# Operands at multiples of 512 bytes, value blocks of 512 columns, and masks in one run, in a two-layer block kernel

## The chip, the cores and the metric

The kernel runs on one core of one Trainium2 chip. The time is the device time of that core in microseconds (us). TensorE (PE in the profile) multiplies, VectorE (DVE) and ScalarE (ACT) do the elementwise work, GpSimd (POOL) a few small operations, and SyncE (SP) issues the transfers. SBUF is the working memory, PSUM the memory that TensorE accumulates in.

## The reference

Two transformer layers over 256 tokens of 1024 features in float32, batch 1. In the first, neighbourhood attention and three-group dilated attention are merged by sigmoid gates, a layer of 16384 experts follows, and a gated embedding. In the second, a multi-scale pooling stands beside differential attention, and a gated convolutional layer ends it.

```python
# first layer
h = rms_norm(x, norm_mix)
qa, ka, va, qd, kd, vd, gate_na, gate_dil = split(h @ w_in)       # va 512 columns, vd 768
out_na = neighbourhood_attention(norm(qa), norm(ka), va, bias)    # 8 heads of 64
out_dil = dilated groups (128,1), (512,4), (2048,16), 4 heads of 64 each, joined by their softmax sums
x = x + (sigmoid(gate_na) * (out_na @ w_na) + sigmoid(gate_dil) * (out_dil @ w_dil)) @ w_out
x = x + peer_ffn(rms_norm(x, norm_ffn))                           # top 16 of 128 x 128 keys, 8 heads; experts u and v
x = x + sigmoid(rms_norm(x, norm_ple) @ w_ple_gate) * (p @ w_ple)
# second layer
p, q, k, v = split(rmsnorm(x) @ w_in_2)
attn = softmax(q1 k1) - lam * softmax(q2 k2)                      # 4 heads of 2 x 64, mask by chunks of 64 tokens
x = x + concat(pool(p), norm(attn @ v)) @ w_o
u = causal_conv(rmsnorm(x) @ w_up); x = x + (silu(u_gate) * u_val) @ w_down
return rmsnorm(x)
```

## The kernel before

All features stand on the 128 partitions, all 256 tokens in one tile. Every weight matrix is cut into units of 128 x 1024 (512 KB), which `Stream` loads in the order of the list `units`. ScalarE copies each to `wh` (rounded to fp32r, `wh<-wr`, L126), and VectorE writes the rest to `wl` (L127). `h_hi`, `h_lo` and their likes are the same two parts of an activation. A product is then three fp32r matmuls: high by high, low by high, high by low (`mm3`, L295 to L297). Where features come out, the activation (256 tokens) is the moving operand and 128 columns of the weights are the stationary one, 24 matmuls of 256 columns for a unit (`feature_unit`). Where tokens come out, the weights move, 512 columns at a time, and the activation is stationary, 12 matmuls for a unit (`token_unit`).

The stages follow each other: value blocks, q and k with the heads behind them, gates, branches and `w_out`, query with the top-16 lists, 128 units of `u` (of which the first 8 take the normalized copy `hP`), 128 units of `v` (stationary operand `av`), the embedding, and the second layer. Work that belongs beside a stage (softmax, transposes, routing) is written as generators, which `Background` steps between units. A scheduler then orders each engine's instructions; `Order` adds edges where the author fixes an order.

**Positions.** A tile takes a multiple of 32 bytes of each partition, and the tiles of a pool stand one behind the other. Worked out from the sizes of the tiles: `x`, `wh`, `wl`, `h_hi`, `h_lo`, `qkd`, `qka`, `vv` and the merged projection's `hp_h` start 352 bytes past a multiple of 512 bytes; `av` and the expert stage's `hp_h`, which stand behind the 32-byte tile `sm` (L704), at 384; `mx_h` at 416; `f_h` at 32. Slices of them begin at multiples of 512 bytes within the tile, so all slices of a tile share its position.

**Value blocks** (L571 to L590). Five blocks of 256 columns, two weight units each, accumulate in a tile of `pmm`; ScalarE writes each to `vv`.

**Scores.** `dilated(j)` is one of four heads: a mask of 512 columns is put into PSUM by a bf16 matmul with the identity (L497), and products over 64 rows are added to it (L498 for the first group, 256 keys; L500 for the second and third, 128 keys). Heads 2c and 2c+1 use rows 0 to 63 and 64 to 127. An f32 matmul is two passes in the profile. `neighbourhood(hp)` makes two heads' scores (L540) without a mask matmul, `differential(h)` those of two softmaxes (L1010), each followed by the chunk mask (L1011).

Of the kernel before, what the change touches and what calls it, by code (L numbers as in the profile page):

```python
# [9 lines left out]
F32 = mybir.dt.float32  # L10
# [10 lines left out]
P = 128  # L21
S = 256
# [151 lines left out]
class Order:  # L174
# [11 lines left out]

    def begin(self):
        self.close()
        self.start, self.last = len(self.nc.cur_bb.bb.instructions), {}
# [32 lines left out]
def block_kernel(ctx, tc, nc, a, out, dbg=None):  # L222
# [12 lines left out]

    x = keep.tile([P, 2, D], F32, name="x")
# [23 lines left out]
    nc.vector.tensor_copy(identb, ident)  # L260

# [49 lines left out]
    def rms_rstd(pool):  # L311

        ss = pool.tile([P, 2, 2], F32, name="ss")
        rstd = pool.tile([P, 2], F32, name="rstd")
# [121 lines left out]
    with ExitStack() as ph:  # L436
# [52 lines left out]
        def dilated(j):  # L489
            po, cj = 64 * (j % 2), j // 2  # L490
            yield from pause(PA)
            row = slice(po, po + 64)
            sc = scores()
            for qt in range(2):
                q = slice(qt * P, (qt + 1) * P)
                o = sc[:, qt * 512:(qt + 1) * 512]
                MM(o, lhsT=identb, rhs=mask[:, qt, :], start=True, stop=False)  # L497
                MM(o[:, :S], lhsT=qkd[row, 0, cj, q], rhs=qkd[row, 1, cj, :], start=False, stop=False)  # L498
                for g in (1, 2):
                    MM(o[:, (g + 1) * P:(g + 2) * P], lhsT=qkd[row, 0, 2 * g + cj, q], rhs=qkd[row, 1, 2 * g + cj, q], start=False, stop=g == 2)  # L500
            yield
            mx = wk.tile([P, 8], F32, name="mx")
# [28 lines left out]
        def neighbourhood(hp):  # L531
# [5 lines left out]
            for i in range(4):  # L537
                hh, qt = divmod(i, 2)
                po = 64 * hh
                MM(sc[:, i * S:(i + 1) * S], lhsT=qka[po:po + 64, 0, hp, qt * P:(qt + 1) * P],  # L540
                   rhs=qka[po:po + 64, 1, hp, :], start=True, stop=True)
# [3 lines left out]
            mx = wk.tile([P, 12], F32, name="mxn")  # L545
# [26 lines left out]
        for i in range(5):  # L572
            ps = pmm.tile([P, 2, S], F32, name="mm", tag="mm")
            for kk in range(2):
                w = st.get(None if i or kk else 0)
                for k4 in range(4):
                    k = 4 * kk + k4
                    for t in range(2):
                        MM(ps[:, t, :], lhsT=hT.hi[:, k, t * P:(t + 1) * P], rhs=w.hi[:, k4 * S:(k4 + 1) * S], start=(k == 0 and t == 0), stop=False)
                        MM(ps[:, t, :], lhsT=hT.hi[:, k, t * P:(t + 1) * P], rhs=w.lo[:, k4 * S:(k4 + 1) * S], start=False, stop=False)  # L580
                        MM(ps[:, t, :], lhsT=hT.lo[:, k, t * P:(t + 1) * P], rhs=w.hi[:, k4 * S:(k4 + 1) * S], start=False, stop=k == 7 and t == 1)
                if i == 0 and kk == 0:
                    norm.rest()
            if i == 0:
                rstd = rms_rstd(wk)
            c = (512 + i * S) if i < 3 else (i - 3) * S
            for t in range(2):
                ACT(vv[:, t, c:c + S], ps[:, t, :], AF.Identity, scale=rstd[:, t:t + 1])
            if i == ROWAT:
                run(rescale(wk, token_row(wk, rstd), hP))  # L590
# [7 lines left out]
        for i in range(10):  # L598
            ps = pmm.tile([P, 2, S], F32, name="mm", tag="mm")
            for j in range(2):  # L600
                feature_unit(ps[:, j, :], st.get(), hP)
                if j == LJ:
                    run(late)
                bg.step(STEPS[0])
            raw = wk.tile([P, 2, S], F32, name="raw", bufs=3)
            ACT(raw, ps, AF.Copy)
            sf = wk.tile([P, 2, S], F32, name="sf")
            ACT(sf, ps, AF.Square)
            sq = HL(wk.tile([P, 2, S], F32R, name="sq_h"), wk.tile([P, 2, S], F32R, name="sq_l"))
            split(sq, sf)  # L610
            if i < 6:
                cj, g = divmod(i, 3)
                jobs = [dilated(2 * cj), dilated(2 * cj + 1)] if g == 2 else []
# [44 lines left out]
    with ExitStack() as ph:  # L658
# [45 lines left out]
        sm = big.tile([P, 8], F32, name="sm")  # L704
# [190 lines left out]
    lam = tab.tile([P, 4], F32, name="lam")  # L895
    lamc = lam[:, 3:4]
    lam_init = 0.8 - 0.6 * float(np.exp(-0.0))
    cmb = tab.tile([P, P], BF, name="cmb")
# [3 lines left out]
    def make_tables():  # L902

        invf = tab.tile([P, 1], F32, name="invf")
# [26 lines left out]
        lj = tab.tile([P, 64], F32, name="lj")  # L931
# [55 lines left out]
    with ExitStack() as ph:  # L987
# [14 lines left out]
        def differential(h):  # L1002
            yield from pause(D0)
            base = psc.tile([P, 2, 512], F32, name="sc")
            for qt in range(2):
                e = P * (qt + 1)
                sc = base[:, :, qt * P:qt * P + e]
                for n in range(2):
                    po = 64 * n
                    MM(sc[:, n, :], lhsT=qk[po:po + 64, 0, h, qt * P:(qt + 1) * P], rhs=qk[po:po + 64, 1, h, :e], start=True, stop=False)  # L1010
                    MM(sc[:, n, e - P:], lhsT=identb, rhs=cmb, start=False, stop=True)  # L1011
            yield
            attn = []
            for qt in range(2):
                e = P * (qt + 1)
                sc = base[:, :, qt * P:qt * P + e]
                mx = wk.tile([P, 8], F32, name="mxd")
# [25 lines left out]
            s2 = wk.tile([P, 4], F32, name="s2")  # L1043
# [57 lines left out]
        def rows2():  # L1101
# [6 lines left out]
            rstd = wk.tile([P, 2], F32, name="rstdn")  # L1108
# [38 lines left out]
    with ExitStack() as ph:  # L1147
# [50 lines left out]
        ss = big.tile([P, 2, 2], F32, name="ss_out")  # L1198
        rstd = big.tile([P, 2], F32, name="rstd_out")
# [37 lines left out]
def _blocks(w):  # L1237

    n = w.shape[1]
    return w.reshape(2, 4, P, n // S, S).transpose(3, 0, 2, 1, 4).reshape(n // S * 2, P, 4 * S)  # L1240
# [6 lines left out]
def _arrays(i):  # L1247
# [8 lines left out]
    d["w_v"] = np.concatenate([_blocks(sp[5]), _blocks(sp[2])])  # L1256
# [81 lines left out]
```

## Time and profile before

| | us |
|---|---|
| three runs | 1369.22, 1370.15, 1371.18; median 1370.15 |
| profiled execution, its own time | 1369.19 |
| its span, first to last instruction | 1367.4 |
| TensorE busy | 1352.7 |
| VectorE busy | 1011.0 |
| ScalarE busy | 744.7 |

Busy time counts overlapping instructions once. Matmuls overlap, so the listed length of one is longer than its distance to the next; the distance is read from two starts in the timeline. `PEld` is the loading of stationary operands.

### The profile page before, as it was taken

To read this page: it belongs to the slowest core of one execution; us is meant where nothing else is said; L and a number is where in the kernel's file an instruction comes from. 1 tells how busy PE (TensorE), PEld (TensorE's weight loads), DVE (VectorE), ACT (ScalarE), POOL (GpSimd) and SP (SyncE) were. 2 spreads that over 40 slices of the span, in tenths; PEclk is the share of its full clock that TensorE was granted. 3 is DMA by queue.
4 is the path that set the end of the run, shared out by engine and by line. 5 is a ranking of instruction groups with operands and counts; after the bars stand their busy time and mean duration, and the time that the engine had idled before them with its cause. 6 is when DMAs were issued, how large, how long until landed. Compare 5 with 4: busy or idle time off the path is not lost.

```text
span 1367.4 us, 23920 instructions
## 1 busy us (share of the span) xinstructions
PE 1352.7 (99%) x9312; PEld 1229.9 (90%) x9312; DVE 1011.0 (74%) x1850; ACT 744.7 (54%) x1293; POOL 10.4 (1%) x16
## 2 busy tenths in 40 slices
PE   9999999999999999999999999999999999999997
PEld 8988998999999999999988888888888788999997
DVE  7687557987889988889855555555557686798886
ACT  6657565564545555544544444444446764665554
POOL 0000000000000000000000000000000000000000
PEclk9999999999999999999999999999999999999999
DMA  6534455455555444454555555555575544455551
GB/s 248 186 120 141 151 163 186 147 184 185 184 185 164 157 159 155 157 168 154 166 188 185 185 187 189 192 186 186 188 248 176 173 148 139 165 190 186 187 185 60
DMA packets 66642, 236.03 MB, mean 173 GB/s; under 512 B 7521, under 2 KB 8545, under 8 KB 66401
## 3 DMA queue, kind: packets, MB, share of 16 engines
q1 hardware_dynamic: 66240, 234.32, 52.5%
q8 instruction: 73, 1.20, 0.3%
q14 instruction: 41, 0.33, 0.1%
q10 hardware_dynamic: 288, 0.18, 0.0%
HBM read 233.43 MB, written 1.05 MB: 171 GB/s over the span
## 4 chain that ended last, share of the span: by engine, by line
PE 78%; DVE 2%; ACT 1%; issue 1%; DMA 0%; POOL 0%; POOLq 0%; DVEq 0%; ACTq 0%
PE acc L295 17%; PE acc L297 17%; PE acc L296 17%; PE mm L295 5%; PE mm L297 5%; PE mm L296 5%; PE up L295 3%; PE up L296 3%; PE up L297 3%; PE trg L831 2%; DVE wl L127 1%; PE sc L1010 1%; PE trs L723 1%; ACT wh L126 0%; DMA wr<-in_w_qk_dram 0%
## 5 line engine op out<-in xcount | busy, mean ns | idle before, releaser
L127 DVE TENSOR_TENSOR wl<-wr,wh 128x1024 fp32r<-128x1024 f32 (+2 forms) x435 | 527.3, 1215 | 263.7 <-ACT wh L126 263.4
L126 ACT ACTIVATE wh<-wr 128x1024 fp32r<-128x1024 f32 (+2 forms) x435 | 457.0, 1053 | 460.8 <-PE acc L297 214.7
L295 PE MATMUL acc<-wh,av 128*128 128x512 f32 x512 | 202.7, 396 | 0.0
L296 PE MATMUL acc<-wl,av 128*128 128x512 f32 x512 | 202.5, 396 | 0.0
L297 PE MATMUL acc<-wh,av 128*128 128x512 f32 x512 | 202.5, 395 | 0.0
L295 PE MATMUL acc<-h_hi,wh 128*128 128x256 f32 x640 | 184.9, 289 | 0.6 <-ACT wh L126 0.6
L297 PE MATMUL acc<-h_hi,wl 128*128 128x256 f32 x640 | 181.1, 283 | 0.3 <-DVE wl L127 0.3
L296 PE MATMUL acc<-h_lo,wh 128*128 128x256 f32 x640 | 181.0, 283 | 0.0
L295 PE MATMUL mm<-h_hi,wh 128*128 128x256 f32 x512 | 147.1, 287 | 1.5 <-ACT vp L1094 1.5
L296 PE MATMUL mm<-h_lo,wh 128*128 128x256 f32 x512 | 145.4, 284 | 0.2
L297 PE MATMUL mm<-h_hi,wl 128*128 128x256 f32 x512 | 144.9, 283 | 0.4 <-DVE wl L127 0.4
L295 PEld LDWEIGHTS acc<-h_hi,wh 128*128 128x128 f32 x640 | 122.5, 191 | 0.8 <-ACT wh L126 0.8
L297 PEld LDWEIGHTS acc<-h_hi,wl 128*128 128x128 f32 x640 | 122.3, 191 | 0.5 <-DVE wl L127 0.5
L296 PEld LDWEIGHTS acc<-h_lo,wh 128*128 128x128 f32 x640 | 122.5, 191 | 0.0
L295 PEld LDWEIGHTS acc<-wh,av 128*128 128x128 f32 x512 | 96.2, 188 | 23.3
L297 PEld LDWEIGHTS acc<-wh,av 128*128 128x128 f32 x512 | 96.2, 188 | 23.3
L296 PEld LDWEIGHTS acc<-wl,av 128*128 128x128 f32 x512 | 96.2, 188 | 23.0
L295 PE MATMUL up<-h_hi,wh 128*128 128x256 f32 x352 | 99.6, 284 | 0.5 <-ACT row L369 0.5
L295 PEld LDWEIGHTS mm<-h_hi,wh 128*128 128x128 f32 x512 | 98.0, 191 | 1.9 <-ACT vp L1094 1.7
L297 PE MATMUL up<-h_hi,wl 128*128 128x256 f32 x352 | 99.5, 283 | 0.0
L296 PE MATMUL up<-h_lo,wh 128*128 128x256 f32 x352 | 99.4, 283 | 0.0
L296 PEld LDWEIGHTS mm<-h_lo,wh 128*128 128x128 f32 x512 | 98.1, 192 | 0.6 <-DVE h_lo L354 0.6
(334 smaller groups left out, 2577.9 us busy)
## 6 DMA issues: line engine op xcount, KB each, us to landing
wr<-in_u_dram SPq DMA_DIRECT2D x128, 512.0 KB, 3.5
wr<-in_v_dram SPq DMA_DIRECT2D x128, 512.0 KB, 3.4
wr<-in_w_up_dram SPq DMA_DIRECT2D x44, 512.0 KB, 3.5
wr<-in_w_down_dram SPq DMA_DIRECT2D x22, 512.0 KB, 3.5
wr<-in_w_q_dram SPq DMA_DIRECT2D x20, 512.0 KB, 4.0
wr<-in_w_g_dram SPq DMA_DIRECT2D x16, 512.0 KB, 3.5
wr<-in_w_query_dram SPq DMA_DIRECT2D x16, 512.0 KB, 3.5
wr<-in_w_v_dram SPq DMA_DIRECT2D x9, 512.0 KB, 4.9
```

Source lines behind the costliest of these rows:

```text
L126: self.last = [self.nc.scalar.activation(hi[:, c], r[:, c], AF.Copy).ins, self.nc.vector.tensor_tensor(lo[:, c], r[:, c], hi[:, c].bitcast ...
L127: self.nc.vector.tensor_tensor(lo[:, c], r[:, c], hi[:, c].bitcast(F32), op=OP.subtract).ins]
L295: MM(o, lhsT=l.hi, rhs=r.hi, start=start, stop=False)
L296: MM(o, lhsT=l.hi, rhs=r.lo, start=False, stop=False)
L297: st.product = MM(o, lhsT=l.lo, rhs=r.hi, start=False, stop=stop).ins
L723: MM(p[:, t, j, :], lhsT=qT[:, 2 * i + j, t * P:(t + 1) * P], rhs=kT[:, j, :], start=True, stop=True)
L831: MM(p[:, j, :], lhsT=o[:, 0, j // 2, :, j % 2], rhs=o[:, k, j // 2, :, j % 2], start=k == 2, stop=k == 3)
L1010: MM(sc[:, n, :], lhsT=qk[po:po + 64, 0, h, qt * P:(qt + 1) * P], rhs=qk[po:po + 64, 1, h, :e], start=True, stop=False)
```

## The change

- `even` takes a whole 512 bytes for a small tile and hands out its front; a pool `t1` holds the small tiles of the first stage; `sums` replaces `sm`; two unused tiles named `room` fill up `cst` and `t1`. Worked out from the sizes, the matmul operands named above all start at multiples of 512 bytes then. `ident` (128), `ones` (64) and `identb` (96) stay.
- The value columns come in three blocks of 512, 256 and 512 columns, in tiles of the scores' PSUM pool; a unit of a 512-column block holds two k-slices. `w_v` is cut to match.
- `dilated(cj)` makes the scores of two heads: first the four mask matmuls, then the products, alternating between rows 0 to 63 and 64 to 127. `in_turn` fixes that order. The rest of each head becomes a job of its own, and both jobs start at once.
- `neighbourhood` and `differential` alternate in the same way; in `differential` the four chunk masks come behind the products.

```diff
+    def in_turn(self, ins):
+        for i, j in zip(ins, ins[1:]):
+            self.edge(j.ins, i.ins)
...
+    def even(pool, shape, name, dtype=F32, bufs=None):
+        t = pool.tile([P, 512 // (4 if dtype in (F32, U32) else 2)], dtype, name=name, **({} if bufs is None else {"bufs": bufs}))
+        n = int(np.prod(shape))
+        v = t[:, :n]
...
+    sums = cst.tile([P, 8], F32, name="sums")
+    cst.tile([P, 32], F32, name="room")
...
+        tiny = ph.enter_context(tc.tile_pool(name="t1", bufs=2))
+        tiny.tile([P, 24], F32, name="room")
...
-        def dilated(j):
-            po, cj = 64 * (j % 2), j // 2
+        def dilated(cj):
             yield from pause(PA)
-            row = slice(po, po + 64)
-            sc = scores()
+            both = [scores() for _ in range(2)]
+            ins = []
+            for qt in range(2):
+                for sc in both:
+                    ins.append(MM(sc[:, qt * 512:(qt + 1) * 512], lhsT=identb, rhs=mask[:, qt, :], start=True, stop=False))
             for qt in range(2):
                 q = slice(qt * P, (qt + 1) * P)
-                o = sc[:, qt * 512:(qt + 1) * 512]
-                MM(o, lhsT=identb, rhs=mask[:, qt, :], start=True, stop=False)
-                MM(o[:, :S], lhsT=qkd[row, 0, cj, q], rhs=qkd[row, 1, cj, :], start=False, stop=False)
-                for g in (1, 2):
-                    MM(o[:, (g + 1) * P:(g + 2) * P], lhsT=qkd[row, 0, 2 * g + cj, q], rhs=qkd[row, 1, 2 * g + cj, q], start=False, stop=g == 2)
+                for g in range(3):
+                    for h, sc in enumerate(both):
+                        row = slice(64 * h, 64 * h + 64)
+                        o = sc[:, qt * 512:(qt + 1) * 512]
+                        o, keys = (o[:, :S], slice(0, S)) if g == 0 else (o[:, (g + 1) * P:(g + 2) * P], q)
+                        ins.append(MM(o, lhsT=qkd[row, 0, 2 * g + cj, q], rhs=qkd[row, 1, 2 * g + cj, keys], start=False, stop=g == 2))
+            order.in_turn(ins)
             yield
+            rest = [dilated_rest(2 * cj + h, sc) for h, sc in enumerate(both)]
+            for job in rest:
+                bg.add(job)
+                next(job)
...
-        for i in range(5):
-            ps = pmm.tile([P, 2, S], F32, name="mm", tag="mm")
-            for kk in range(2):
+        for i, (c, n) in enumerate(((512, 512), (1024, 256), (0, 512))):
+            ps = scores()
+            per = 1024 // n
+            for kk in range(KD // per):
                 w = st.get(None if i or kk else 0)
...
-        sm = big.tile([P, 8], F32, name="sm")
+        sm = sums
...
-                    MM(sc[:, n, e - P:], lhsT=identb, rhs=cmb, start=False, stop=True)
+                    ins.append(MM(sc[:, n, :], lhsT=qk[po:po + 64, 0, h, qt * P:(qt + 1) * P], rhs=qk[po:po + 64, 1, h, :e], start=qt == 0, stop=False))
+            for qt in range(2):
+                for n in range(2):
+                    ins.append(MM(base[:, n, 2 * qt * P:(2 * qt + 1) * P], lhsT=identb, rhs=cmb, start=False, stop=qt == 1))
+            order.in_turn(ins)
```

Two places show how TensorE's order moves. The first is the dilated scores of heads 0 and 1 in the q and k stage (`mm` is the projection that the scores stand in, `sc` the scores, `identb` the identity that each mask loads). Before, in the second of two stretches, TensorE has:

```order
L295 MATMUL mm<-hp_h,wh 128x256
L500 MATMUL sc<-qkd 128x128
L497 LDWEIGHTS identb
L497 MATMUL sc<-mask,identb 128x512
L498 MATMUL sc<-qkd 128x256
L500 MATMUL sc<-qkd 128x128 x3
L497 LDWEIGHTS identb
L497 MATMUL sc<-mask,identb 128x512
L498 MATMUL sc<-qkd 128x256
L500 MATMUL sc<-qkd 128x128 x2
L296 MATMUL mm<-hp_l,wh 128x256
```

In the changed program the same stretch, on the same engine, reads:

```order
L313 MATMUL mm<-hp_h,wl 128x256
L525 MATMUL sc<-qkd 128x128 x2
L525 MATMUL sc<-qkd 128x256 x2
L525 MATMUL sc<-qkd 128x128 x4
L311 MATMUL mm<-hp_h,wh 128x256
```

Both masks have left this stretch for the first one, where four pairs of `LDWEIGHTS identb` and the mask matmul now stand behind each other, ahead of two products of 256 and two of 128 columns. The first row of scores here is the third group's. Between the two stretches there were 22 matmuls `mm` before and there are 18 now.

The second place is a differential head's scores in the second layer's q and k stage (`cmb` is the chunk mask). Before, TensorE has:

```order
L295 MATMUL mm<-h_hi,wh 128x256
L1010 MATMUL sc<-qk 128x128
L1011 LDWEIGHTS identb
L1011 MATMUL sc<-cmb,identb 128x128
L1010 MATMUL sc<-qk 128x128
L1011 LDWEIGHTS identb
L1011 MATMUL sc<-cmb,identb 128x128
L1010 MATMUL sc<-qk 128x256
L1011 LDWEIGHTS identb
L1011 MATMUL sc<-cmb,identb 128x128
L1010 MATMUL sc<-qk 128x256
```

In the changed program the same head reads:

```order
L311 MATMUL mm<-h_hi,wh 128x256
L1045 MATMUL sc<-qk 128x128 x2
L1045 MATMUL sc<-qk 128x256 x2
L1048 LDWEIGHTS identb
L1048 MATMUL sc<-cmb,identb 128x128
```

The products of the two softmaxes, one on each half of the rows, now follow each other, and the four masks, of which the first is shown, come behind them.

## Rows read from the trace of the kernel before

**Rows 1.** The page, part 1: engine, busy us (share of the span) and instructions.

```profile
...
PE 1352.7 (99%) x9312; PEld 1229.9 (90%) x9312; DVE 1011.0 (74%) x1850; ACT 744.7 (54%) x1293; POOL 10.4 (1%) x16
```

**Rows 2.** Waits of TensorE, longest total first: who waited for whom, us, times, longest.

```profile
...
PE mm L295 <- ACT vp L1094: 1.5, 1, 1.5
```

**Rows 3.** Groups by line and shape on TensorE: count, then busy us, mean ns.

```profile
...
L295 PE MATMUL acc<-wh,av 128*128 128x512 f32 x512 | 202.7, 396 | 0.0
...
L295 PE MATMUL acc<-h_hi,wh 128*128 128x256 f32 x640 | 184.9, 289 | 0.6 <-ACT wh L126 0.6
...
L295 PE MATMUL mm<-h_hi,wh 128*128 128x256 f32 x512 | 147.1, 287 | 1.5 <-ACT vp L1094 1.5
...
L295 PE MATMUL up<-h_hi,wh 128*128 128x256 f32 x352 | 99.6, 284 | 0.5 <-ACT row L369 0.5
...
L295 PE MATMUL mm<-hp_h,wh 128*128 128x256 f32 x320 | 92.2, 288 | 0.0
```

**Rows 4.** Timeline of TensorE, 256 columns: start us, us, then the instruction.

```profile
...
286.65 0.28 PE L295 MATMUL acc<-hp_h,wh 128*128 128x256 f32 x1
...
297.96 0.28 PE L295 MATMUL mm<-hp_h,wh 128*128 128x256 f32 x1
...
320.89 0.28 PE L295 MATMUL acc<-h_hi,wh 128*128 128x256 f32 x1
...
332.41 0.28 PE L295 MATMUL mm<-h_hi,wh 128*128 128x256 f32 x1
```

**Rows 5.** Timeline of TensorE, 512 columns, two places.

```profile
...
202.26 0.39 PE L295 MATMUL acc<-wh,hp_h 128*128 128x512 f32 x1
...
203.62 0.28 PE L295 MATMUL mm<-ona_h,wh 128*128 128x256 f32 x1
203.73 0.28 PE L296 MATMUL mm<-ona_l,wh 128*128 128x256 f32 x1
...
900.07 0.40 PE L297 MATMUL acc<-wh,av 128*128 128x512 f32 x1
...
903.57 0.40 PE L297 MATMUL acc<-wh,av 128*128 128x512 f32 x1
```

**Rows 6.** Timelines of TensorE and VectorE, scores of the dilated and neighbourhood heads.

```profile
...
66.87 0.39 PE L497 MATMUL sc<-mask,identb 128*128 128x512 bf16 x1
67.19 0.70 PE L498 MATMUL sc<-qkd 64*128 64x256 f32 x2
67.72 0.38 PE L500 MATMUL sc<-qkd 64*128 64x128 f32 x2
...
69.20 0.39 PE L295 MATMUL mm<-hp_h,wh 128*128 128x256 f32 x1
...
72.02 0.49 PE L500 MATMUL sc<-qkd 64*128 64x128 f32 x2
...
75.22 0.39 PE L296 MATMUL mm<-hp_l,wh 128*128 128x256 f32 x1
...
126.90 1.14 PE L540 MATMUL sc<-qka 64*128 64x256 f32 x8
...
70.76 0.68 DVE L484 TENSOR_TENSOR qkd<-qn,r 128x512 f32<-128x512 f32 x1
```

**Rows 7.** Timeline of TensorE, scores of one differential head.

```profile
...
1102.34 0.46 PE L1010 MATMUL sc<-qk 64*128 64x128 f32 x2 [0.17 <-issue]
1102.73 0.23 PE L1011 MATMUL sc<-cmb,identb 128*128 128x128 bf16 x1
...
1103.47 0.70 PE L1010 MATMUL sc<-qk 64*128 64x256 f32 x2
1104.10 0.23 PE L1011 MATMUL sc<-cmb,identb 128*128 128x128 bf16 x1
...
1104.92 0.36 PE L296 MATMUL mm<-h_lo,wh 128*128 128x256 f32 x1
```

**Rows 8.** A window of the query stage, columns as in its first line.

```profile
...
core 0: us, PE busy (x) PEld busy (x) DVE busy (x) ACT busy (x) POOL busy (x), PEclk, DMA share, GB/s
228.00:287.00 59.00, 58.61 (x488) 58.15 (x489) 55.35 (x204) 37.42 (x59) 0.74 (x1) 1.00 0.49 161
```

More of the change, by code (lines that the diff above doesn't have):

```diff
@@ L309, in in_order, with rms_rstd @@
         return ap.rearrange("p (n t) -> p n t", t=2)
-    def rms_rstd(pool):
-        ss = pool.tile([P, 2, 2], F32, name="ss")
-        rstd = pool.tile([P, 2], F32, name="rstd")
+    def rms_rstd(pool, small_pool=None):
+        if small_pool is not None or isinstance(pool, type):
+            own = small_pool or pool
+            ss, rstd = own.tile([P, 2, 2], F32, name="ss"), own.tile([P, 2], F32, name="rstd")
+        else:
+            ss, rstd = even(pool, (2, 2), "ss"), even(pool, (2,), "rstd")
         for n in range(2):
@@ L536, in neighbourhood @@
             sc = scores()
[L537 to L541, printed above, removed]
+            ins = []
+            for qt in range(2):
+                for hh in range(2):
+                    i, po = 2 * hh + qt, 64 * hh
+                    ins.append(MM(sc[:, i * S:(i + 1) * S], lhsT=qka[po:po + 64, 0, hp, qt * P:(qt + 1) * P],
+                                  rhs=qka[po:po + 64, 1, hp, :], start=True, stop=True))
+            order.in_turn(ins)
             yield
@@ L571, in block_kernel @@
         hP = mT = HL(big.tile([P, KD, S], F32R, name="hp_h"), big.tile([P, KD, S], F32R, name="hp_l"))
-        for i in range(5):
-            ps = pmm.tile([P, 2, S], F32, name="mm", tag="mm")
-            for kk in range(2):
+        for i, (c, n) in enumerate(((512, 512), (1024, 256), (0, 512))):
+            ps = scores()
+            per = 1024 // n
+            for kk in range(KD // per):
                 w = st.get(None if i or kk else 0)
-                for k4 in range(4):
-                    k = 4 * kk + k4
+                for kw in range(per):
+                    k, cw = per * kk + kw, slice(kw * n, (kw + 1) * n)
                     for t in range(2):
-                        MM(ps[:, t, :], lhsT=hT.hi[:, k, t * P:(t + 1) * P], rhs=w.hi[:, k4 * S:(k4 + 1) * S], start=(k == 0 and t == 0), stop=False)
-                        MM(ps[:, t, :], lhsT=hT.hi[:, k, t * P:(t + 1) * P], rhs=w.lo[:, k4 * S:(k4 + 1) * S], start=False, stop=False)
-                        MM(ps[:, t, :], lhsT=hT.lo[:, k, t * P:(t + 1) * P], rhs=w.hi[:, k4 * S:(k4 + 1) * S], start=False, stop=k == 7 and t == 1)
+                        mm3(ps[:, t * 512:t * 512 + n], hT[:, k, t * P:(t + 1) * P], w[:, cw], k == 0, k == 7)
                 if i == 0 and kk == 0:
                     norm.rest()
+                if i == 0 and kk == 1:
+                    rstd = rms_rstd(wk, tiny)
+            for t in range(2):
+                ACT(vv[:, t, c:c + n], ps[:, t * 512:t * 512 + n], AF.Identity, scale=rstd[:, t:t + 1])
             if i == 0:
[L585 to L589, printed above, removed]
                 run(rescale(wk, token_row(wk, rstd), hP))
@@ L612, in block_kernel @@
                 cj, g = divmod(i, 3)
-                jobs = [dilated(2 * cj), dilated(2 * cj + 1)] if g == 2 else []
+                jobs = [dilated(cj)] if g == 2 else []
                 late = heads(raw, sq, qkd[:, :, 2 * g + cj, :], QK_DIL, True, jobs)
@@ L1004, in differential @@
             base = psc.tile([P, 2, 512], F32, name="sc")
+            ins = []
             for qt in range(2):
@@ L1009, in differential @@
                     po = 64 * n
-                    MM(sc[:, n, :], lhsT=qk[po:po + 64, 0, h, qt * P:(qt + 1) * P], rhs=qk[po:po + 64, 1, h, :e], start=True, stop=False)
-                    MM(sc[:, n, e - P:], lhsT=identb, rhs=cmb, start=False, stop=True)
+                    ins.append(MM(sc[:, n, :], lhsT=qk[po:po + 64, 0, h, qt * P:(qt + 1) * P], rhs=qk[po:po + 64, 1, h, :e], start=qt == 0, stop=False))
+            for qt in range(2):
+                for n in range(2):
+                    ins.append(MM(base[:, n, 2 * qt * P:(2 * qt + 1) * P], lhsT=identb, rhs=cmb, start=False, stop=qt == 1))
+            order.in_turn(ins)
             yield
@@ L1042, in differential @@
             yield
-            s2 = wk.tile([P, 4], F32, name="s2")
+            s2 = even(wk, (4,), "s2")
             on = wk.tile([P, 2, P], F32, name="on")
```

34 lines of the change are left out of this document (20 added, 14 removed).

## The prediction

> **What bounds the kernel now.** I read the page first, for the engine that is never idle. TensorE is busy 1352.7 us of the span, VectorE 1011.0 [rows 1]. The waits of TensorE come next: the largest entry is 1.5 us in all, in one wait [rows 2]. So the time is the number of matmuls multiplied by the distance from one start to the next, plus the places where TensorE changes its tiling. Busy time does not give that distance, since matmuls overlap: a 256-column matmul is listed with some 285 ns. The timeline does. In the expert stage, 96 matmuls (four units of 24) start between 320.89 and 332.41, which is 120.0 ns each [rows 4]. In the second expert stage fifteen 512-column matmuls take 3.50 us, or 233.3 ns [rows 5]. At the granted clock of 1.00 (the 2.4 GHz level, [rows 8]) the columns alone would take 106.7 and 213.3 ns, so 13 to 20 ns of every matmul are something else.
>
> **Part 1, the positions.** The matmuls do not all have that distance, and the groups differ in nothing but where their operands lie:
> - 256 columns, moving and stationary operand both at 352 past a multiple of 512 bytes: 120.0 ns.
> - 256 columns, moving operand (hP of the second stage) at 384, stationary at 352: 96 matmuls from 286.65 to 297.96, or 117.8 ns [rows 4].
> - 512 columns, moving 352, stationary (av) 384: 233.3 ns.
> - 512 columns, both at 352 (merged projection): six from 202.26 to 203.62, or 227 ns [rows 5].
>
> So position counts. The change puts both operands at 0, a pair that the trace does not hold, and the price must be bounded. For 512 columns the nearest row is the pair with equal positions, 227; the ends are 233.3 (no effect) and 220. For 256 columns the nearest is the pair whose moving operand is a multiple of 128, 117.8; the ends are 120.0 and 113, the distance of the first 256-column matmul behind a 512-column run (203.62 to 203.73, [rows 5]). The 220 is an estimate: the same 6.3 ns over the columns that 113 leaves at 256 columns, 213.3 + 6.3. I take the nearest rows.
> - The 512-column matmuls with av are 3 x 512 [rows 3]: 1536 x (233.3 - 227) = 9.7 us; at the ends 0 and 20.4.
> - The 256-column ones with h and hP: 3 x (640 + 512 + 352 + 320) [rows 3] less the 96 at 384 = 5376, x (120.0 - 117.8) = 11.8 us; at the ends 0 and 37.6. Smaller groups are left out.
>
> The Trainium skill speaks against this part. TensorE: Matmul & The Clock Gate, "Step-by-step: what each phase is for", says that the moving operand and the weight load have read ports of their own, so that loading the next weights takes nothing from the running matmul. By that rule both terms are 0, which is rival A. The trace does not agree: 227 against 233.3 at one width and one moving position.
>
> **Part 2, the value blocks.** Five blocks of 256 columns, two units of 24 matmuls each, cost 240 x 120.0 = 28.8 us. After: 96 of 512 columns and 48 of 256, 96 x 227 + 48 x 117.8 = 27.5. That is -1.3 (bounds: -0.6 with 233.3 and 120.0, -2.3 with 220 and 113). The weight units arrive at the same pace, 512 KB per block-half of some 2.8 us, and the h columns are wanted later than before; waits at the start count as 0.
>
> **Part 3, the scores.** Alternating halves buys nothing by itself. In the neighbourhood heads the program has both matmuls of one half, then both of the other, and yet the 8 passes (two for each f32 matmul) take 1.14 us [rows 6]; two passes of 256 columns alone take 0.53 (67.19 to 67.72). The halves already run side by side when nothing stands between. Price of that edit: 0. What separates the heads in the dilated and differential scores is the mask: it uses all rows, so each one closes both halves. The gain is in taking the masks out from between.
> - Dilated, first stretch, before: 66.87 to 69.20 = 2.33 us for two times mask (0.32), 256 columns (0.53) and 128 columns with the way out (0.32). After, four masks in one run and the halves together: three masks at about 0.22 (an estimate between the bare 0.213 and 0.227), one at 0.32, then 0.53 + 0.32 once = 1.83.
> - Dilated, second stretch, before: 72.02 to 75.22 = 3.20. After: 128 columns 0.32, 256 columns 0.43 (0.53 without the 0.10 by which a mask in front of a change of tiling is longer, 0.32 against 0.22), then twice 128 columns, about 0.22 and 0.32: 1.3. Together 2.4 us for a pair of heads.
> - But the third group's q and k are written by VectorE from 70.76 on for 0.68, until 71.44 [rows 6]. Before, TensorE asks for them at 72.02. After, it has saved 0.5 and does 18 instead of 22 matmuls between, so it asks at about 70.9 and waits some 0.5 us. What is queued behind it is the rest of the q and k stage. Net 1.9 a pair, two pairs: 3.8 us (bounds 2 and 5).
> - Differential, before: 1102.34 to 1104.92 = 2.58 us a head. After: the 128-column passes without their way out 0.29, the 256-column passes until the mask (1103.47 to 1104.10) 0.63, four masks in one run about 0.25 = 1.17 [rows 7]. 1.4 x 4 heads = 5.6 us (bounds 4 and 7).
>
> All of it lies on TensorE, which waits nowhere in these stages, so it is taken off the end. The softmax of both dilated heads now begins together, on VectorE and ScalarE, whose results TensorE wants some units later; priced 0.
>
> **The sum.** 9.7 + 11.8 + 1.3 + 3.8 + 5.6 = 32.2 us. The profiled execution has a span of 1367.4 and a time of 1369.2, so 1.8 lie around the span; after: 1335.2 + 1.8 = 1337.0. It was 1.0 below the median of the runs, 1370.15, which gives 1338. Does another engine take over? The nearest is the query stage, where VectorE is busy 55.35 of 59.00 us [rows 8]. At 117.8 the stage shrinks by 1.9% to 57.9, and VectorE still fits.
>
> **Rivals.**
> - A: the positions do nothing at 0. What speaks for it: 117.8 and 227 come from pairs of other positions. Then only the masks and the wider blocks stay, 3.8 + 5.6 + 0.6 = 10.0: 1360.
> - C: both at 0 is the good pair, 113 and 220. For it: 113 is seen, so the array can do it. Against: in the trace it holds for one matmul and is back at 120 within three. Time: 20.4 + 37.6 + 2.3 + 9.4 = 69.7, less some 2 us for VectorE, whose 55.35 would then meet 59.00 x 113/120 = 55.6: 1302. Of the same kind is the skill's formula (TensorE: Matmul & The Clock Gate, "Back-to-back issue gap": N/2.4 + 2.5 ns, that is 109.2 and 215.8); with it the sum would give about 1273, an estimate from that page, and no row here is as short.
> - S, the other side: 0 and 0 is a bad pair. The pair 352 and 384 costs 48 columns over its 512 (233.3 x 2.4 = 560), the pair 352 and 352 only 32 over its 256 (288). If all 256-column matmuls fall into the first class they take 304 columns, 126.7 ns: 5376 x 6.7 = +36 us, av stays at 233.3, the masks give 9.4 and the blocks 0.3: 1396. It decides as soon as 256 columns take more than 123.8 ns with av improved (9.7 + 1.3 + 9.4 = 20.4 over 5376). Against it: at 512 columns equal positions are the better class, and equal they stay.
>
> **Chances and range.** Forecast 0.42, C 0.25, A 0.20, S 0.10, the rest 0.03 between and beyond. Predicted: 1338, own range 1322 to 1352 (the 256-column distance between 115 and 120, av at 227). The range that leaves out no more than 2 in 10 drops S and the part of C beyond its own bounds: 1285 to 1362. A measurement of this kernel can tell about 0.2%, 2.7 us: below 1367.4 lie the forecast, A and C, 0.87; within 0.03; above 0.10.
>
> **What would show it.** The start-to-start distances in the two expert stages are the test: 117.8 and 227 in my case, 120.0 and 233.3 in A, 113 and 220 in C, 126.7 in S. The dilated scores should take 1.8 and 1.3 us instead of 2.3 and 3.2, with a wait of TensorE for qkd of about 0.5 in front of the third group; the differential ones 1.2 instead of 2.6; the neighbourhood ones 1.1 as now. I am wrong in the step of part 1 if the distances differ, and in part 3 if those stretches shrink and the stage's end does not come earlier by as much, because a softmax is then what TensorE waits for.

## The result and the profile after

| | us |
|---|---|
| before | median 1370.13 (1369.22 to 1371.18) |
| after, four runs | median 1352.47 (1351.17 to 1353.97) |
| ratio, 95% interval | 0.9871 (0.9854 to 0.9888) |
| forecast | 1338, range 1285 to 1362 |

The kernel is 17.7 us faster; 32.2 were forecast. The four runs follow the clock that TensorE was granted: 1351.17 at a mean of 0.998, 1352.34 and 1352.61 at 0.997, 1353.97 at 0.996, where the trace shows two falls to the lower level ahead of the last microseconds, worth some 1.3 to 1.4 us each. The page of the changed kernel, span and part 1:

```profile
span 1352.2 us, 23723 instructions
...
PE 1332.8 (99%) x9216; PEld 1219.7 (90%) x9216; DVE 1010.5 (75%) x1850; ACT 742.9 (55%) x1289; POOL 10.4 (1%) x16
```

TensorE is still busy 99% of a span that is 15.2 us shorter (the profiled execution, 1353.97, was the slowest of the four). Where the time came from is read in three places. First the groups by line and shape (count, busy us, mean ns), which answer to [rows 3], and the distances in the timeline, which answer to [rows 4, 5]:

```profile
...
L311 PE MATMUL acc<-wh,av 128*128 128x512 f32 x512 | 199.4, 389 | 0.0
```

```profile
...
282.88 0.28 PE L311 MATMUL acc<-hp_h,wh 128*128 128x256 f32 x1
...
294.40 0.28 PE L311 MATMUL mm<-hp_h,wh 128*128 128x256 f32 x1
...
317.08 0.28 PE L311 MATMUL mm<-h_hi,wh 128*128 128x256 f32 x1
...
328.60 0.28 PE L311 MATMUL acc<-h_hi,wh 128*128 128x256 f32 x1
...
888.21 0.39 PE L311 MATMUL acc<-wh,av 128*128 128x512 f32 x1
...
891.61 0.39 PE L311 MATMUL acc<-wh,av 128*128 128x512 f32 x1
```

The `av` matmuls are listed with 389 ns instead of 396, and fifteen of them take 3.40 us: 226.7 ns instead of 233.3. But both stretches of 96 matmuls with 256 columns take 11.52 us, which is 120.0 ns, with `hp_h` as with `h_hi`. Before, they were 117.8 and 120.0. So the positions paid at 512 columns and not at all at 256.

Second the scores (timeline), against [rows 6, 7]:

```profile
...
66.77 1.04 PE L517 MATMUL sc<-mask,identb 128*128 128x512 bf16 x4
67.74 0.92 PE L525 MATMUL sc<-qkd 64*128 64x256 f32 x8
68.59 0.39 PE L311 MATMUL mm<-hp_h,wh 128*128 128x256 f32 x1
...
71.45 1.37 PE L525 MATMUL sc<-qkd 64*128 64x128 f32 x16 [0.44 <-DVE qkd L505]
72.75 0.39 PE L311 MATMUL mm<-hp_h,wh 128*128 128x256 f32 x1
...
127.32 1.14 PE L575 MATMUL sc<-qka 64*128 64x256 f32 x8
...
1091.22 0.93 PE L1045 MATMUL sc<-qk 64*128 64x128 f32 x8
1092.08 0.40 PE L1048 MATMUL sc<-cmb,identb 128*128 128x128 bf16 x4
1092.28 0.36 PE L312 MATMUL mm<-h_lo,wh 128*128 128x256 f32 x1
```

The dilated stretches take 68.59 - 66.77 = 1.82 and 72.75 - 71.45 = 1.30 us (2.33 and 3.20 before), with the wait for `qkd` in front of the second; the neighbourhood one is listed with 1.14 as before; the differential one takes 1.06 instead of 2.58.

Third the second layer's q and k stage, which holds the differential heads, by windows: from the transposes `trr` to the first score, and from there to the first `mx` matmul (length, busy us of PE, PEld, DVE, ACT, POOL, granted clock, DMA share, GB/s). After, and then before:

```profile
...
1073.49:1091.22 17.73, 15.43 (x116) 15.05 (x114) 12.08 (x15) 8.46 (x12) 0.00 (x0) 0.90 0.80 260
1091.22:1128.20 36.98, 35.07 (x286) 31.92 (x286) 31.23 (x85) 23.57 (x68) 2.07 (x3) 1.00 0.39 129
```

```profile
...
1086.70:1102.34 15.64, 13.95 (x115) 13.57 (x114) 11.91 (x15) 8.49 (x12) 0.00 (x0) 1.00 0.84 283
1102.34:1142.77 40.43, 40.27 (x285) 34.89 (x286) 31.52 (x85) 23.52 (x68) 2.07 (x3) 1.00 0.39 123
```

The four heads are 6.2 us shorter in themselves (2.58 to 2.61 before, 1.06 now), yet the second window only loses 40.43 - 36.98 = 3.45, and the first one grows by 2.09, at a granted clock of 0.90. The rows of that are TensorE's waits (who waited for whom, us, times, longest), ScalarE's timeline and TensorE's behind the longest wait:

```profile
...
PE mm L311 <- ACT vp L1132: 2.2, 1, 2.2
...
PE sc L525 <- DVE qkd L505: 1.0, 2, 0.5
...
PE sc L1045 <- DVE qk L1034: 0.5, 2, 0.4
...
PE tra L1068 <- DVE s L1085: 0.5, 1, 0.5
```

```profile
...
1075.94 1.06 ACT L126 ACTIVATE wh<-wr 128x1024 fp32r<-128x1024 f32 x1 [2.69 <-DMA wr<-in_w_qk_dram]
1076.90 0.82 ACT L1132 ACTIVATE vp<-mm,rstdn 128x256 f32<-128x256 f32 x2
```

```profile
...
1077.77 0.38 PE L311 MATMUL mm<-h_hi,wh 128*128 128x256 f32 x1 [2.23 <-ACT vp L1132]
...
1079.65 0.41 PE L312 MATMUL mm<-h_lo,wh 128*128 128x256 f32 x1
...
1082.00 0.41 PE L311 MATMUL mm<-h_hi,wh 128*128 128x256 f32 x1
```

`vp` stands on ScalarE behind a weight copy that waits 2.69 us for its transfer, so TensorE waits 2.23 us for it instead of 1.5 [rows 2]. Behind that wait the granted clock falls to its lower level, 1.2 GHz, for some three microseconds: eleven matmuls from 1079.65 to 1082.00 are 213.6 ns apart. The columns alone take 256 / 1.2 = 213.3 there, so at the lower level nothing beside the columns is left to see.

### The profile page after: what moved, and what is told of

Read it like the earlier page. It is cut to its first block, busy times and chain, and to the rows that moved or that the text cites. A ratio compares the mean times of both kernels' runs of the same rounds, so it can differ in the third digit from the quotient of the medians.

```text
span 1352.2 us, 23723 instructions
## 1 busy us (share of the span) xinstructions
PE 1332.8 (99%) x9216; PEld 1219.7 (90%) x9216; DVE 1010.5 (75%) x1850; ACT 742.9 (55%) x1289; POOL 10.4 (1%) x16
## 4 chain that ended last, share of the span: by engine, by line
PE 76%; DVE 4%; ACT 1%; DMA 1%; issue 1%; POOL 0%; POOLq 0%; ACTq 0%; DVEq 0%
PE acc L311 17%; PE acc L313 17%; PE acc L312 16%; PE mm L311 4%; PE mm L313 4%; PE mm L312 4%; PE up L311 3%; PE up L313 3%; PE up L312 3%; PE trg L865 2%; DVE wl L127 1%; PE trs L757 1%; ACT wh L126 0%; DMA wr<-in_w_ple_gate_dram 0%; DMA wr<-in_w_qk_dram 0%
## 5 line engine op out<-in xcount | busy, mean ns | idle before, releaser
L311 PE MATMUL acc<-wh,av 128*128 128x512 f32 x512 | 199.4, 389 | 0.0
L313 PE MATMUL acc<-wh,av 128*128 128x512 f32 x512 | 199.2, 389 | 0.0
L312 PE MATMUL acc<-wl,av 128*128 128x512 f32 x512 | 199.2, 389 | 0.0
L313 PEld LDWEIGHTS mm<-h_hi,wl 128*128 128x128 f32 x512 | 98.8, 193 | 0.6 <-DVE wl L127 0.6
```

The source lines that it names most:

```text
L311: MM(o, lhsT=l.hi, rhs=r.hi, start=start, stop=False)
L312: MM(o, lhsT=l.hi, rhs=r.lo, start=False, stop=False)
L313: st.product = MM(o, lhsT=l.lo, rhs=r.hi, start=False, stop=stop).ins
```

## The experiments

The changed kernel's own gain is split first (positions, blocks, scores), then the distances are measured by themselves, then the rule that they show is built back into the kernel. Each was timed beside runs of the kernel before (1369.99 to 1370.13).

**Every pair of a few positions, with nothing else running.** 48 matmuls to a group, PSUM tile `ps_` and then q (256 columns) or f (512) and one letter each for the moving and the stationary position, a = 0, b = 32 and so on up to p = 480.

```diff
+    for name, n, m, s in positions():
+        p = ps.tile([P, 512], F32, name="ps_" + name, tag="ps")
+        for i in range(48):
+            k, part = divmod(i, 3)
+            mo, so = 8 * m + n * (k % (2048 // n)), 8 * s + 128 * k
+            MM(p[:, :n], lhsT=sta[part == 2][:, so:so + 128], rhs=mov[part == 1][:, mo:mo + n], start=i == 0, stop=i == 47)
```

> Leaves the whole computation out: 72 groups of 48 fp32r matmuls that wait for nothing, 36 with a moving operand of 256 columns and 36 with one of 512, the moving and the stationary operand each shifted in steps of 32 bytes. Theory R (only the difference of the two positions counts, and no difference is one of the better cases): 0/0 and 352/352 alike, 120 ns for 256 columns and 227 ns for 512; 384/352 at 117.8 for 256 columns, 352/384 at 233 for 512; some other difference is shorter than 120 ns at 256 columns. Rival Z (a multiple of 512 counts by itself): 0/0 shorter than 352/352 at 512 columns by some 6 ns. Rival L (the 13.3 ns beside the columns belong to the change of the stationary operand alone): all groups of 256 columns at 120 within 1 ns.

The view of one tile gives the first and the last start of 16 of the 48 matmuls (lengths ns, then starts us), 45 distances apart:

```profile
L261 PE MATMUL ps_qll<-mh,sh x16: 278/283/283, 188.3 to 193.7; 128*128 128x256 f32 x16
...
L261 PE MATMUL ps_qln<-mh,sh x16: 276/276/279, 205.4 to 210.5; 128*128 128x256 f32 x16
...
L261 PE MATMUL ps_fll<-mh,sh x16: 389/389/398, 561.8 to 572.1; 128*128 128x512 f32 x16
...
L261 PE MATMUL ps_flm<-mh,sh x16: 392/396/396, 584.0 to 594.5; 128*128 128x512 f32 x16
```

352/352 (`ll`) is 5.4 us / 45 = 120 ns, 352/416 (`ln`) 5.1 / 45 = 113; at 512 columns 352/352 is 10.3 / 45 = 229 and 352/384 (`lm`) 10.5 / 45 = 233 (by all starts of a group 119.6, 113.4, 227.7, 233.2). 0/0 had a median of 120.0 at 256 columns, and a mean of 227.5 at 512; 384/352, the pair of `hP` before, had 117.9. Theory R holds in that a multiple of 512 is worth nothing by itself; that equal positions are one of the better cases holds at 512 columns alone. L falls, since 256 columns range from 113.4 to 120.

**The kernel before, with one 32-byte tile moved.**

```diff
+    sums = cst.tile([P, 8], F32, name="sums")
+    cst.tile([P, 120], F32, name="room")
...
-        sm = big.tile([P, 8], F32, name="sm")
+        sm = sums
```

> The kernel before with one edit: the 32-byte tile sm goes to the constants with 480 bytes of filling, so that av and the expert stages' hP stand at 352 like the weights; nothing stands at 0. Theory R (equal positions are enough): av at 227 ns, so 1536 x 6.5 = 10 us less, 0.3 us of it lost with hP; 1370.1 becomes 1360.4. Rival Z (it must be a multiple of 512): av stays at 233.4, 1370 to 1371.

1360.65 us, ratio 0.9933 (0.9919 to 0.9946). Groups by line and shape:

```profile
...
L297 PE MATMUL acc<-wh,av 128*128 128x512 f32 x512 | 199.4, 389 | 0.0
```

`av` is at 389 ns with nothing at a multiple of 512. R, to 0.3 us.

**The changed kernel with the positions of before.**

```diff
-        t = pool.tile([P, 512 // (4 if dtype in (F32, U32) else 2)], dtype, name=name, **({} if bufs is None else {"bufs": bufs}))
...
+        return pool.tile([P] + list(shape), dtype, name=name, **({} if bufs is None else {"bufs": bufs}))
...
-    cst.tile([P, 32], F32, name="room")
...
+        tiny = wk
...
-        sm = sums
+        sm = big.tile([P, 8], F32, name="sm")
```

> The changed kernel with the positions of before (352, 384, 416, 32), the value blocks and the scores as changed. If the positions are worth the 10 us of av and about 0.5 us of the small groups, and nothing at 256 columns: 1352.5 + 10.5 = 1363. If the 256-column matmuls gained something that a shorter stage then gave back elsewhere: above 1365.

1361.00 us, 0.9936 (0.9922 to 0.9949): 9.0 us faster than before without any position, and 8.5 slower than the changed kernel, 2 less than I expected. With the 9.4 of the tile alone, the two parts add up to 18.4, and together they give 17.7.

**The changed kernel with five value blocks.**

```diff
-        for i, (c, n) in enumerate(((512, 512), (1024, 256), (0, 512))):
-            ps = scores()
-            per = 1024 // n
-            for kk in range(KD // per):
+        for i in range(5):
+            ps = pmm.tile([P, 2, S], F32, name="mm", tag="mm")
+            for kk in range(2):
...
```

> The changed kernel with the five value blocks of 256 columns. My account: the wider blocks are worth 1.3 us by the distances, and the fall of the granted clock at 7.9 to 10.5 us (1.2 us) with the waits behind it has eaten that, so that undoing them leaves the time within 1 us of 1352.5, with a granted clock of 1.00 from 0 to 10 us. Rival: the fall has nothing to do with the blocks, stays, and the kernel is 1 to 2 us slower.

1351.79 us, 0.9868 (0.9853 to 0.9883): within 1 us of the changed kernel, as expected. The stretch up to the first matmul with `hP`, with five blocks, with three in the changed kernel, and with three in a kernel whose clock did not fall there (the last one of this section):

```profile
...
0.00:39.66 39.66, 37.24 (x274) 35.52 (x275) 27.01 (x43) 24.68 (x42) 0.91 (x5) 1.00 0.69 250
```

```profile
...
0.00:39.52 39.52, 36.09 (x179) 30.17 (x180) 27.28 (x43) 23.21 (x38) 0.90 (x5) 0.96 0.71 245
```

```profile
...
0.00:38.14 38.14, 35.75 (x178) 30.13 (x179) 27.29 (x43) 23.21 (x38) 0.90 (x5) 1.00 0.73 255
```

The granted clock is 1.00 with five blocks against 0.96, and at 1.00 the three blocks are done 1.5 us earlier. So the distances give what they promised (1.3), and in the changed kernel the fall takes it back. At the end no gain of the blocks is shown: the medians are 0.7 us apart in favour of five, the fastest runs 0.06. Nor is the fall the blocks' own: it also stands in the kernel with one tile moved, which has five blocks (0.85 from 10 to 20 us), and not in the kernel with the weights moved, below, which has three (1.00). What brings it on at the start stays open.

**The whole table.** All 16 x 16 pairs in a shuffled order, a matmul of 128 columns ahead of each group.

```diff
-        for i in range(48):
+        count = 36 if n == 256 else 18
+        MM(p[:, :128], lhsT=sta[0][:, :128], rhs=mov[0][:, :128], start=True, stop=True)
+        for i in range(count):
...
+    return [r[i] for i in np.random.RandomState(7).permutation(len(r))]
```

> Leaves the whole computation out: all 16 x 16 pairs of positions (moving, stationary, in steps of 32 bytes) at 256 columns (36 matmuls each) and at 512 (18 each), in a shuffled order, with one matmul of 128 columns ahead of each group. If the distance is a function of the pair and not of what ran before: the pairs of the first table come out within 0.5 ns of it (0/64, 64/0, 352/416 and 352/32 at 113.4 for 256 columns; 0/0 and 0/256 at 227 for 512), whatever stands ahead. Rival: 113.4 is a state that one group hands to the next, since in the first table 352/32 ran right behind 352/416; then 352/32 is found elsewhere, near 118.

Mean distance in ns, from the fifth matmul of a group to its last, over the 32 pairs of each difference (left out is one 512-column group, the first to run, most of which had the lower clock):

| stationary minus moving, mod 256 | 256 columns: mean, least, most | 512 columns: mean, least, most |
|---|---|---|
| 0 | 119.9, 119.6, 120.0 | 227.5, 226.7, 228.6 |
| 32 | 118.3, 118.2, 118.4 | 233.2, 232.6, 233.3 |
| 64 | 115.4, 113.3, 117.8 | 233.3, 233.3, 233.7 |
| 96 | 118.0, 117.3, 120.0 | 234.3, 233.8, 234.6 |
| 128 | 119.0, 118.6, 120.0 | 232.8, 231.7, 233.3 |
| 160 | 120.0, 119.8, 120.0 | 233.6, 233.3, 234.2 |
| 192 | 117.1, 113.3, 117.9 | 228.9, 228.8, 228.9 |
| 224 | 116.9, 116.5, 117.8 | 233.3, 233.2, 233.5 |

What the distance follows is the difference of the two positions, modulo 256, whatever they are themselves. At 512 columns each difference has one value within 2 ns, and equal is the best. At 256 columns equal and 160 are the worst, and 64 is the best. But 64 has two values, about 113.4 (17 of the 32 pairs) and 117.8, and 192 has them too (113.4 in 5); 96, 128 and 224 spread by 1.3 to 2.7. 0/64 and 64/128 in the view of one tile, 33 distances each:

```profile
L256 PE MATMUL ps_qac<-mh,sh x12: 276/276/332, 410.9 to 414.7; 128*128 128x256 f32 x12
...
L256 PE MATMUL ps_qce<-mh,sh x12: 281/281/332, 1224.0 to 1228.0; 128*128 128x256 f32 x12
```

That is 3.8 / 33 = 115 with the slower first ones in it, and 4.0 / 33 = 121; by the distances from the fifth on 113.3 and 117.8. So the expectation was half wrong: 352/32 and 64/0, both a difference of 192, came out at 117.8 and not at 113.4. But the rival's reason does not hold either: in the first table 352/32 ran right behind 352/416 (113.4), but 64/0 ran behind 32/0 (116.8); and here two groups of difference 64 or 192 right behind one at 113.3 had 117.8. What chooses between the two values was not found.

**The weights 64 bytes further on.** `wh` and `wl` at 64, all else of the changed kernel in its place.

```diff
+        self.shifted = []
...
+            if pool not in self.shifted:
+                pool.tile([P, 16], F32, name="room", bufs=1)
             hi = pool.tile([P, 1024], F32R, name="wh", tag="wh")
             lo = pool.tile([P, 1024], F32R, name="wl", tag="wl")
+            if pool not in self.shifted:
+                pool.tile([P, 112], F32, name="rest", bufs=1)
+                self.shifted.append(pool)
```

> The changed kernel with wh and wl 64 bytes further on, all else in its place. Theory R2 (at 256 columns equal positions are the worst class, and a difference of 64 bytes costs 6.6 ns less): some 5500 matmuls of 256 columns at 113.4 instead of 120 give 36 us, the 512-column ones at 64/0 take 229 instead of 227 and give 4 us back; 1352.5 becomes 1320, or up to 6 us more where VectorE or a transfer then ends last. Rival: the short distance holds only in a loop that nothing else disturbs; 118 in the kernel, some 11 less and 4 more, 1345.

1341.63 us (1338.31 to 1345.92), 0.9791 (0.9777 to 0.9805): 10.8 faster than the changed kernel, nearer the rival's 1345 than the 1320 of R2. The 256-column matmuls of the experts have a mean of some 115.6 ns, a mixture of the two values, and the runs lie 7.6 us apart. `av` fell back, and the dilated heads wait longer for q and k:

```profile
...
L317 PE MATMUL acc<-wh,av 128*128 128x512 f32 x512 | 203.6, 398 | 0.0
...
PE sc L531 <- DVE qkd L511: 2.1, 2, 1.3
```

398 ns is the old class (233.4 apart), where the table has 228.9 for this difference (192). The products with `f` stand at the same difference and took 230.6. So at 192 the table does not carry over to every product of the kernel; why `av` is slower there was not found.

**One tile of 64 bytes ahead of the weights**, so that `h` alone stays at 0 and `av` goes with the weights.

```diff
         self.raw_pool = ctx.enter_context(tc.tile_pool(name="wraw", bufs=raw_bufs))
+        self.raw_pool.tile([P, 16], F32, name="room", bufs=1)
```

> The changed kernel with one tile of 64 bytes ahead of the weights: h stays at 0, the weights and all that stands behind them (av, f, mx, hP) at 64. Theory R2 (the difference decides, at 256 columns 0 is the worst class and 64 the best, at 512 columns 0 is the best): av stays at 227; the 256-column matmuls with h go to what they were in the kernel with the weights alone moved (115.6 in 3456, 117.6 in 1056: 15.1 + 2.5 = 17.6 us), those with hP stay at 120; 1335. Rival Z (multiples of 512 count): av goes back to 233, and nothing at 256 columns improves; 1362.

1338.75 us, 0.977 (0.9757 to 0.9783). `av` is at 226.8, so R2 and not Z. The experts' 256 columns came out at 116.6 instead of 115.6; over some 2730 distances that is 2.7 of the 3.7 us that are missing.

**The same with `hP` at a multiple of 512.**

```diff
-        hP = mT = HL(big.tile([P, KD, S], F32R, name="hp_h"), big.tile([P, KD, S], F32R, name="hp_l"))
+        hP = mT = HL(*(big.tile([P, 112 + KD * S + 16], F32R, name=n)[:, 112:112 + KD * S].rearrange("p (a b) -> p a b", a=KD) for n in ("hp_h", "hp_l")))
```

> The same, with hP of the q and k stage put at a multiple of 512 again, so that it too differs from the weights by 64: 864 further matmuls at 115 instead of 120, 4 us, 1331; the merged projection's 96 at 229 instead of 227 cost 0.2. Rival: the dilated heads wait for q and k by as much longer (1.3 instead of 0.5 us where this was so), and 2 us at most are left.

1336.31 us, 0.9755 (0.9742 to 0.9768): the fastest version, 33.8 us ahead of the kernel before and 16.2 ahead of the changed one. 48 matmuls in the experts and 18 in the up projection:

```profile
...
315.69 0.28 PE L312 MATMUL acc<-h_hi,wh 128*128 128x256 f32 x1
...
321.13 0.28 PE L312 MATMUL acc<-h_hi,wh 128*128 128x256 f32 x1
...
1200.66 0.28 PE L312 MATMUL up<-h_hi,wh 128*128 128x256 f32 x1
...
1202.78 0.28 PE L312 MATMUL up<-h_hi,wh 128*128 128x256 f32 x1
```

5.44 / 48 = 113.3 ns in the one place and 2.12 / 18 = 117.8 in the other, at the same positions: the two values again, now in the kernel. Of the 4 us of `hP`, 2.4 reached the end, near the rival's 2; the wait for `qkd` is 2.1 us in all instead of 1.0.

**Halves one after the other**, masks in one run as changed.

```diff
-                for g in range(3):
-                    for h, sc in enumerate(both):
+                for h, sc in enumerate(both):
+                    for g in range(3):
```

The same swap of the two loops stands in the neighbourhood and the differential heads.

> The changed kernel with the products of one half of the rows first and then those of the other, in all three kinds of heads; masks in one run as changed. My step (alternating buys nothing, the masks out of the way buy it): dilated stretches of 1.8 and 1.3 us, differential ones of 1.06, neighbourhood ones of 1.06, and 1352.5 within 1.5. Rival (the alternation is what makes the halves run side by side): dilated 2.3 and some 1.9, differential 1.7, and 5 us slower.

1352.72 us, 0.9873 (0.9858 to 0.9888): by the medians no difference, but the granted clock was not the same (a mean of 0.997 to 0.999 here, of 0.996 to 0.998 in the changed kernel). Timeline of the dilated and a differential head (the first of the four masks has no record, so that the stretch began some 0.2 us ahead of 66.91):

```profile
...
66.91 0.81 PE L517 MATMUL sc<-mask,identb 128*128 128x512 bf16 x3
67.65 0.92 PE L525 MATMUL sc<-qkd 64*128 64x256 f32 x4
68.50 0.39 PE L311 MATMUL mm<-hp_h,wh 128*128 128x256 f32 x1
...
71.56 2.23 PE L525 MATMUL sc<-qkd 64*128 64x128 f32 x20
...
73.73 0.50 PE L490 MATMUL tr<-sq_h,bones 128*128 128x512 f32 x1
...
1092.79 0.93 PE L1045 MATMUL sc<-qk 64*128 64x128 f32 x8
...
1093.86 0.36 PE L312 MATMUL mm<-h_lo,wh 128*128 128x256 f32 x1
```

The differential head takes 1.07 us as with alternation. The dilated ones are not quite alike: in the first stretch only head 0 has products before it needs the third group's, so the second stretch is 2.17 instead of 1.30, but TensorE does not wait ahead of it. The q and k stage with its heads, from the first matmul with `hP` to the first with `ona`, in the kernel before, in the changed one and in this one:

```profile
...
39.57:184.59 145.02, 145.01 (x1119) 132.54 (x1118) 98.73 (x152) 95.03 (x178) 0.00 (x0) 1.00 0.45 144
```

```profile
...
39.52:180.73 141.21, 140.22 (x1117) 128.62 (x1116) 98.58 (x152) 94.92 (x178) 0.00 (x0) 1.00 0.47 150
```

```profile
...
39.43:182.78 143.35, 142.11 (x1115) 130.65 (x1116) 97.97 (x152) 96.03 (x178) 0.00 (x0) 1.00 0.44 148
```

At the same granted clock the stage is 2.1 us longer without alternation. The two dilated pairs explain some 0.4 us each, and a wait of 0.6 us of the neighbourhood scores for `pr`, which the changed kernel does not have, more of it; the rest was not traced. So alternating buys nothing for running side by side, but is worth about 2 us in this stage for what it lets go early. In the profiled executions, both with two falls of the clock, 1.6 of it are left at the end (1355.55 against 1353.97).

**The differential scores of before.**

```diff
-                    ins.append(MM(sc[:, n, :], lhsT=qk[po:po + 64, 0, h, qt * P:(qt + 1) * P], rhs=qk[po:po + 64, 1, h, :e], start=qt == 0, stop=False))
...
-            order.in_turn(ins)
+                    MM(sc[:, n, :], lhsT=qk[po:po + 64, 0, h, qt * P:(qt + 1) * P], rhs=qk[po:po + 64, 1, h, :e], start=True, stop=False)
+                    MM(sc[:, n, e - P:], lhsT=identb, rhs=cmb, start=False, stop=True)
```

> The changed kernel with the differential scores of before (a mask behind each product, 2.6 us a head instead of 1.06). If the 6.2 us saved there reach the end: 1358.7. If they are given back in the stage (a longer wait for vp, the fall of the clock behind it, waits for softmax and qk), as the trace of the changed kernel suggests, in which the stage is 1.8 us shorter and not 6.7: 1354, and these waits are gone.

1354.75 us, 0.9892 (0.9877 to 0.9907). So by the medians 2.3 of the 6.2 us saved in the four heads reach the end, near my account. The first two windows as above:

```profile
...
1072.05:1088.53 16.48, 13.94 (x115) 13.56 (x114) 12.08 (x15) 8.34 (x12) 0.00 (x0) 1.00 0.83 277
1088.53:1128.98 40.45, 40.31 (x285) 34.93 (x286) 31.52 (x85) 23.59 (x68) 2.07 (x3) 1.00 0.34 117
```

The second window is back at 40.45, and TensorE has no wait in it that the trace lists, against 1.8 us in five kinds of waits with the new scores: these waits come with the shorter scores. The window's length gives the gain free of the clock: 40.45 - 36.98 = 3.5 us; the other 0.9 us is in no listed wait. That is also what lies between the runs at a granted clock of 0.998 (1354.72 to 1354.77 in three of the four here, 1351.17 in the changed kernel). The wait for `vp` is 2.5 us here too, so it is not the differential scores that make it longer, and that part of my account falls. And there the clock stays at 1.00 behind it, so the wait alone does not bring the fall.

## Why the prediction was right in direction and short in size

The measured 1352.5 lies at the slow edge of the prediction's own range (1322 to 1352), the edge that it set at 120 ns for 256 columns and 227 for 512; that is what came.

**What bounds the kernel** held: TensorE's distances set the time, and every change of them that was measured came out at the end, up to the waits named.

**Part 1, 512 columns** (forecast 9.7): right. 1536 x (233.4 - 226.8) = 10.1 us in the trace, 9.4 when done alone. The reason was half seen: equal positions are the good class at this width, and the change made them equal. That they became multiples of 512 added nothing.

**Part 1, 256 columns** (forecast 11.8): this is the step that failed. The prediction put it as "For 256 columns the nearest is the pair whose moving operand is a multiple of 128, 117.8". Of the row's two differences I took the wrong one: `hP` was better because it stood 32 bytes off the weights, not because 384 is a multiple of 128. The table has 116.9 for that difference (stationary minus moving = -32, that is 224; some 117.8 in 7 of its 32 pairs) and 119.9 for none. The change removed the difference, so the experts' 192 matmuls of `hP` went from 117.8 to 120.0 and the others stayed. The row that would have told it stood in [rows 4] itself: at 352/352 the positions were already equal, and the distance was 120.0. I had used equality as the reason at 512 columns and not at 256.

The Trainium skill, TensorE: Matmul & The Clock Gate, "Step-by-step: what each phase is for", has it that weight loads have a read port of their own and take nothing from the running matmul. The runs speak against it for these fp32r matmuls: with the same instructions the distance moves from 113.3 to 120.0 ns with the difference of the two operands' positions, so the two reads are not free of each other; what they share is not shown. The formula of its section "Back-to-back issue gap", which the section gives for the isolated gap, makes 109.2 and 215.8 ns; the shortest means of any pair here were 113.3 and 226.7.

**Part 2, the blocks** (1.3): the distances gave 1.5 where the clock stayed up (38.14 against 39.66), but that nothing happens at the start did not hold: in the profiled execution a fall of the clock took it back, and by the medians five blocks are 0.7 us faster, inside the spread of both.

**Part 3, dilated** (3.8 for two pairs): right in its pieces. 1.83 and 1.3 were forecast, 1.82 and 1.30 measured, and the wait for `qkd` of about 0.5 a pair came as 1.0 for two; the whole stage is 145.02 - 141.21 = 3.8 shorter. The price 0 for alternating held for the halves running side by side (1.06 and 1.07 us in the neighbourhood heads), but not for the stage, where it is worth 2.1.

**Part 3, differential** (5.6): the heads gave 6.2, but their stage became only 3.5 shorter. I had priced what follows at nothing ("taken off the end"); in fact the softmax and the next q and k are then late, which TensorE meets as waits, 1.8 us in the profiled execution. The 0.7 more for `vp` ahead of the stage is not the new scores' doing, since it came with the old ones too (2.5 us); nor do they always bring the 1.4 at the lower clock behind that wait, which the kernel with five value blocks and the new scores does not have.

The 15.2 us between the spans of the profiled executions can be added up from the forecast. Of 32.2 us the 11.8 did not come, and from the first matmul with `ona` to the first with `av` the kernel is 0.6 longer instead (0.4 of it `hP`); 2.7 went to two falls of the clock, 0.7 to the longer wait for `vp`, 2.1 of the 5.6 were given back. On the other side stand 0.4 more for `av`, and 0.5 for the stage of the 96 matmuls with `mx`, which I had left out (medians of 233 and 227 ns): 32.2 - 17.9 + 0.9 = 15.2. The medians show 17.7, since not every run had both falls. Rival A (no position counts, 1360) is the kernel with the positions of before, 1361.0; rival S fell, as did C for these positions: its 113 exists, but at a difference of 64.

## What to carry to other kernels

Where matmuls follow each other without a wait, read the distance of starts and set it against the two operands' positions: what counted here was their difference modulo 256 bytes, and the best difference was another at 256 columns (64) than at 512 (0). Measure it in the kernel too: at a difference of 192 `av` took 233.4 ns where the loop had 228.9. Align to what the pair wants, not to a round number; one tile of 64 bytes was worth 13.7 us on top of the whole change. A saving on the engine that sets the end is only worth what the next operand's arrival leaves of it, so price the wait that comes next. And where the gain is as small as one fall of the clock (1.3 to 1.4 us here), compare stages by their lengths in the traces, at the same granted clock.

## What was not expected of the hardware

- At 2.4 GHz a 256-column matmul took 113.3 to 120.0 ns by the positions; at the lower level 213.6, nothing beside its 213.3 of columns. The 512-column group of the table that ran at the lower level, at a difference of 96, took 427, with 426.7 of columns. In these two rows, what the positions cost is there at the higher level only.
- At the difference 64 the same instructions run at 113.4 or at 117.8 for long stretches; what chooses is open, and in the one kernel the runs lay 7.6 us apart.
- The clock fell behind a wait of 2.2 us for `vp` in the changed kernel, and not behind one of 2.5 in the kernel with the differential scores of before or of 2.7 in the one with a tile of 64 bytes.
